# Keeping mixer tokens column by column of the grid, so that a neighbourhood attention reads 160 keys instead of 256

## The chip, the cores and the metric

The kernel runs on one core of one Trainium2 chip. The metric is the device time of one execution in microseconds (us). A time is the median of several runs; one further execution is taken by the hardware profiler, and what is read below of single instructions comes from that one.

## What is computed

Two layers of an encoder on 256 tokens of width 2048, all in 32-bit floats. Each layer has a mixing part with two attentions and a convolutional feed-forward part. Cut to what matters here:

```python
SEQ, GRID_W, NA_KH, NA_KW, WIN = 256, 64, 8, 16, 128     # 4 rows x 64 columns of tokens
h = rmsnorm(x, norm_mix[l]) * (1.0 + sc_a) + sh_a
qa, ka, va, qb, kb, vb, ga, gb = split_cols(h @ w_in[l])
ya = window_attention(qa, ka, va, sink_a[l]) @ w_proj_a[l]        # mixer A: |i - j| <= 128, with a sink
yb = neighbourhood_attention(qb, kb, vb, rel_bias_b[l]) @ w_proj_b[l]   # mixer B
merged = jax.nn.sigmoid(ga) * ya + jax.nn.sigmoid(gb) * yb
x = x + gt_a * (merged @ w_out[l])
# ... rmsnorm, w_up, depthwise conv over neighbouring tokens, silu gate, w_down
```

In mixer B (8 heads of 128) a query sees all 4 rows of the grid, and of the 64 columns a window of 16 that is moved inwards at the edges. A token's number is row * 64 + column. So in the usual order of tokens the keys that one query sees lie in four pieces, and every tile of 128 queries sees all 256 keys.

## The kernel before

**What streams.** Every weight matrix is cut into blocks of 128 x 128, and 16 blocks make a unit (1 MB, one DMA into a `raw` buffer). ScalarE (ACT) rounds each half unit to a high part (L326) and VectorE (DVE) subtracts it for the low part (L327); both land in an `hl` buffer. TensorE (PE) multiplies each block three times (high x high, high x low, low x high): `feature_block` (L343 to L345) with 256 tokens as moving columns, `tokens` (L406 to L408) with 512 output columns. Beside this stream the conditioning vectors are computed on DVE from `aw` tiles of 1 MB (L233). All DMAs of inputs are issued by one queue, SP, in program order: an issue that waits for a buffer holds back those behind it.

**The part around the change.** `normed` makes `h`, the normalised and modulated input, chunk by chunk (DVE L497, ACT L500, DVE L501), each chunk as high and low parts. From `h` come q, k, v of both mixers (`packs`) and the gates. A generator `attention` runs the 16 heads in steps between the matmuls of the stream; its pace is set by rates per unit. One head (`attend`) is: scores on PE into PSUM (L651); mask or bias added and the row's maximum taken on DVE (L654); exponential, sum and scaling on ACT (L662, L670); the probabilities turned so that keys lie on partitions; split into high and low parts (L418, L421); the sums of values on PE (L689); and the output split again (L691, L692). In layer 0 the scores are plain f32 matmuls and the turning is four PE transposes (L681) into PSUM. In layer 1 the scores are three split matmuls, and the turning is one DVE transpose of 32 x 32 blocks (L304), after which GpSimd (POOL) moves 16 blocks per head to their places (L298). For mixer B the tile `p` is first the bias, loaded by one DMA of 256 KB (L880), and then the probabilities. `merge` (L1011 to L1015) adds the gated outputs of both mixers and splits the sum; from there `w_out`, the residual and the feed-forward part follow. The pool `ev` has three buffers of the tag `z`, which `ht` in `normed` and `m` in `merge` use in turn.

**What sets the order.** The program is recorded in one go and a scheduler places the instructions of each engine by priorities and dependencies; each engine then runs its own in order. A few instructions are pinned in place (`keep_in_program_order`).

Of the kernel before, what the change touches and what calls it, by code (L numbers as in the profile page):

```python
# [9 lines left out]
F32 = mybir.dt.float32  # L10
F32R = mybir.dt.float32r
AF = mybir.ActivationFunctionType
# [3 lines left out]
P = 128  # L16
L = 2
D = 2048
S = 256
# [67 lines left out]

MOVED_QK = [(), (0,1,2,8)]
QK_STEPS = 3
MOVED = [(0,0), (8,8)]  # L90
STEPS = [1, 1]

ADA_ORDER = [[p * KC + k for k in range(KC) for p in ps] for ps in ((0, 1), (2,), (3, 4), (5,))]
# [48 lines left out]
def encoder(ctx: ExitStack, tc: tile.TileContext, a: dict, out: bass.AP):  # L142
# [43 lines left out]
    skip(96, const)  # L186
    skip(224)
    sp = pool("s", 1)

    def place(tag, n, dt, name):  # L190
        return sp.tile([P, n, S], dt, name=name, tag=tag)
# [110 lines left out]
    def turned_blocks(src, rows, n):  # L302
# [3 lines left out]
        dst = src.rearrange("p t (n k) -> p (t n k)", n=n).rearrange("p (n t k) -> p n t k", n=n, t=2)  # L306
        moved_blocks(dst, blocks)

    def unit_steps(l, u, by_halves=False):

        raw = rawp.tile([P, UB * P], F32, name=f"w{l}_{u}", tag="raw")
        if not by_halves:
            nc.sync.dma_start(raw[:], a["ws"][l, u])
        halves = []
        streamed = any(m == "w_in" and mo < GATE_A // P for m, _, mo in STREAMS[l][u * UB : (u + 1) * UB])
        at = OFF if streamed else 0
        for j in range(2):
            n = UB * P // 2  # L320
            hl = hlp.tile([P, 2 * n + ROW], F32R, name=f"hl{l}_{u}_{j}", tag="hl")
            hl = hl[:, at : at + 2 * n].rearrange("p (a n) -> p a n", a=2)
            r = raw[:, j * n : (j + 1) * n]
            if by_halves:
                nc.sync.dma_start(r, a["ws"][l, u][:, j * n : (j + 1) * n])
            nc.scalar.copy(hl[:, 0], r)  # L326
            nc.vector.tensor_tensor(out=hl[:, 1], in0=r, in1=hl[:, 0].bitcast(F32), op=ALU.subtract)  # L327
            halves.append(hl)
            if j == 0:
                yield halves  # L330
# [84 lines left out]
    def split(dst, src, scale=None, held=False):  # L415
# [9 lines left out]
            out=dst[:, 1], in0=src, scalar=scale, in1=dst[:, 0].bitcast(F32), op0=ALU.mult, op1=ALU.subtract  # L425
        )

    def half_tanh(dst, src, **kw):

        nc.scalar.activation(out=dst, in_=src, func=AF.Tanh, scale=0.5, **kw)  # L430
# [60 lines left out]
    def normed(l, w, h, rbs):  # L491

        mod, amod = mods[l], amods[l]
        for kc in range(KC):
            t = ev.tile([P, S], F32, name="ht", tag="z")
            sh = mod[:, 3 * w * KC + kc : 3 * w * KC + kc + 1]
            nc.vector.scalar_tensor_tensor(  # L497
                out=t[:], in0=x[:, kc], scalar=amod[:, w, kc : kc + 1], in1=rbs[:], op0=ALU.mult, op1=ALU.mult
            )
# [145 lines left out]

    def attend(q, k, v, p, mask, scale, sink, o, rows=None):

        sc = ax.tile([P, 2, S], F32, name="sc", tag="ax")
        for t in range(2):
            for i, j in by(q):  # L650
                nc.tensor.matmul(sc[:, t], q[i][:, t * P : (t + 1) * P], k[j], start=i + j == 0, stop=(i, j) == by(q)[-1])  # L651
        m = sm.tile([P, 2], F32, name="m", tag="m")
        for t in range(2):
            nc.vector.tensor_tensor_reduce(  # L654
                out=p[:, t], in0=sc[:, t], in1=mask[:, t], scale=scale, scalar=-3.0e38 if sink is None else sink,
                op0=ALU.add, op1=ALU.max, accum_out=m[:, t : t + 1],
            )
        nm = sm.tile([P, 2], F32, name="nm", tag="nm")
        nc.vector.tensor_scalar(out=nm[:], in0=m[:], scalar1=-1.0, scalar2=None, op0=ALU.mult)
        den = sm.tile([P, 2], F32, name="den", tag="den")  # L660
        for t in range(2):
            nc.scalar.activation(out=p[:, t], in_=p[:, t], func=AF.Exp, bias=nm[:, t : t + 1], accum_out=den[:, t : t + 1])  # L662
        if sink is not None:
            es = sm.tile([P, 2], F32, name="es", tag="es")
            nc.scalar.activation(out=es[:], in_=nm[:], func=AF.Exp, bias=sink)
            nc.vector.tensor_tensor(out=den[:], in0=den[:], in1=es[:], op=ALU.add)
        ri = sm.tile([P, 2], F32, name="ri", tag="ri")
        nc.vector.reciprocal(out=ri[:], in_=den[:])
        for t in range(2):
            nc.scalar.activation(out=p[:, t], in_=p[:, t], func=AF.Copy, scale=ri[:, t : t + 1])  # L670
        yield
        if rows is not None:
            turned_blocks(p[:], rows(), 2)
            for _ in range(STEPS[sink is None]):
# [8 lines left out]
        split(pT, tp[:], held=rows is not None)  # L683
        v = v()
        yield
        po = ax.tile([P, 512], F32, name="po", tag="ax")
        for i, j in by(v):
            for b in range(2):
                nc.tensor.matmul(po[:, :S], v[i][:, b], pT[:, j, b], start=i + j + b == 0, stop=i + b == 2)  # L689
# [96 lines left out]
    def small(l):  # L786

        if l == 0:
            tables.extend((load(a["maskA"], [P, 2, S], "maskA"), load(a["cs"], [P, 2, 2, HALF], "cs")))
        cs = tables[1]  # L790
        gains = load(a["gains"][l], [P, 4], f"gains{l}", lay, tag="gains", bufs=1)
        rg = load(a["rg"][l], [P, 2, ROT], f"rg{l}", lay, tag="rg", bufs=1)
        sink = load(a["sink"][l], [P, HA], f"sink{l}", lay, tag="sink", bufs=1)
        cw = load(a["cw"][l], [P, 2 * FC, 4], f"cw{l}", lay, tag="cw", bufs=1)
        nc.vector.tensor_scalar(out=gains[:, 2:3], in0=gains[:, 2:3], scalar1=SCALE, scalar2=None, op0=ALU.mult)
        rots = []
        for w in range(2):
            rot = lay.tile([P, 4, 2, HALF], F32, name=f"rot{l}_{w}", tag=f"rot{w}", bufs=1)
            for i, (f, g) in enumerate(((0, 0), (1, 1), (0, 1), (1, 0))):
                nc.vector.tensor_tensor(  # L800
                    out=rot[:, i], in0=cs[:, f],
                    in1=rg[:, w, g * HALF : (g + 1) * HALF].unsqueeze(1).broadcast_to([P, 2, HALF]), op=ALU.mult,
                )
            rots.append(rot)

        return gains, sink, cw, rots

    for l in range(L):
# [17 lines left out]
        if l:  # L826


            def bare_gate(mo):
                def evac(ps):  # L830
                    z, sh = bare.level(ps, 0.5)
                    half_tanh(ya[:, mo], z[:], bias=sh[:, :1])
# [17 lines left out]
        def head_a(i):  # L850
# [21 lines left out]
            yield from attend(  # L872
                q, k, v, p, tables[0], SCALE, sink[:, i : i + 1], lambda: oA[i], rows if i < MOVED[l][0] else None
            )

        def head_b(hb):
            b, i = packs[1 + hb // 4], hb % 4
            v = b[:, 4:8].rearrange("p (t a) s -> p t (a s)", t=2)
            p = at.tile([P, 2, S], F32, name="p", tag="p")
            nc.sync.dma_start(p[:], a["bias"][l, hb])  # L880
            q = in_halves(b[:, 8 + i], f"qB{l}_{hb}", "qh", l in SCORES_3)
            k = in_halves(b[:, i], f"kB{l}_{hb}", "kh", l in SCORES_3)
            yield
            yield from attend(
                q, k, lambda: in_halves(v[:, :, i * HEAD : (i + 1) * HEAD], f"vB{l}_{hb}", "vh", True), p, p, 1.0, None,
                lambda: oB_of(hb), (lambda: b[:, i : 9 + i : 8]) if hb < MOVED[l][1] else None,
            )

        def oB_of(hb):
# [119 lines left out]
        for mo in range(KC):  # L1009

            def merge(ps):  # L1011
                z = ev.tile([P, S], F32, name="m", tag="z")
                gated(z[:], gb[mo], ps)
                nc.vector.tensor_tensor(out=z[:], in0=z[:], in1=ya[:, mo], op=ALU.add)
                split(merged[mo], z[:], 0.5)  # L1015

            st.features(oB, [merge])

# [185 lines left out]
```

## Time and profile before

| | |
|---|---|
| time, median of 3 runs | 2653.98 us (2653.2 to 2656.04) |
| profiled execution, its own time | 2661.45 us |
| its span, first to last instruction | 2659.6 us |
| TensorE clock granted | 1.000 of full speed |
| busy: PE, DVE, ACT, POOL | 99%, 80%, 53%, 9% of the span |
| DMA | 700.42 MB, 70.8% of 16 engines' time for the SP queue |

The profiled execution is 7.5 us above the median of the plain runs, and 1.85 us of its time lie outside the span. A row of a group gives line, engine, operation, tiles and shapes, count, then busy time in us, mean ns of one, and the idle time just before with its cause. In the timeline a row gives start, duration, engine and line; where several instructions were merged, the count stands at the end. The duration of one matmul is longer than the distance to the next, since matmuls overlap: their price is the distance of starts. The profile records each plain f32 matmul as two (32 rows for the 16 f32 score matmuls of the 8 B heads in layer 0).

### The profile page before, as it was taken

Reading aid. Unit: us, or ns where it says so; the run is one execution under the profiler, and the core shown is the slowest. Engines: PE = TensorE matmul, PEld = TensorE weight load, DVE = VectorE, ACT = ScalarE, POOL = GpSimd, SP = SyncE. Lnnn points to the kernel's source line nnn. Section 1 sums busy time; section 2 is a strip of 40 time slices with the busy share of each in tenths; the row PEclk is TensorE's granted clock in tenths of the full one; section 3 lists DMA queues with packets and bytes.
Section 4 is the critical chain, followed back from the end, with each engine's and each line's share of the span. In section 5 each row is a group of like instructions: output and inputs, shape, how many; then the busy total and the mean of one; then the engine's idle time right before and its main releaser. Section 6 shows DMA issues by size and latency. Waiting matters only on the chain.

```text
span 2659.6 us, 51014 instructions
## 1 busy us (share of the span) xinstructions
PE 2643.3 (99%) x21164; PEld 2557.9 (96%) x21164; DVE 2121.0 (80%) x2979; ACT 1408.9 (53%) x2280; POOL 228.2 (9%) x345
## 2 busy tenths in 40 slices
PE   9999999999999999999999999999999999999999
PEld 7888899999999999999998889999999999999999
DVE  8898998997987888788886778868888866655664
ACT  5445865456643555355554666654565445544553
POOL 0001100000000000000002558520000000000000
PEclk9999999999999999999999999999999999999999
DMA  9987779885777777877766666666747765555554
GB/s 371 349 329 292 267 294 356 316 339 184 295 272 289 284 287 285 306 296 285 283 221 253 249 234 232 253 258 257 283 178 287 297 252 191 192 196 194 196 191 143
DMA packets 102042, 700.42 MB, mean 263 GB/s; under 512 B 12721, under 2 KB 15025, under 8 KB 17969
## 3 DMA queue, kind: packets, MB, share of 16 engines
q1 hardware_dynamic: 101810, 697.17, 70.8%
q8 instruction: 165, 2.70, 0.4%
q14 instruction: 67, 0.55, 0.1%
HBM read 695.03 MB, written 2.10 MB: 262 GB/s over the span
## 4 chain that ended last, share of the span: by engine, by line
PE 86%; DMA 5%; DVE 5%; issue 2%; ACT 1%; POOL 0%; SPq 0%; DVEq 0%; ACTq 0%
PE ps L343 24%; PE ps L345 24%; PE ps L344 24%; DMA aw<-in_aw 4%; PE ps_t L408 4%; PE ps_t L407 4%; PE ps_t L406 4%; DVE hl L327 2%; DVE aw L233 1%; PE sc L651 1%; ACT hl L326 1%; PE po L689 1%; DMA w<-in_ws 1%; DVE u L1049 0%; POOL qrs L472 0%
## 5 line engine op out<-in xcount | busy, mean ns | idle before, releaser
L327 DVE TENSOR_TENSOR hl<-w,hl 128x1024 fp32r<-128x1024 f32 x928 | 1129.8, 1224 | 298.0 <-ACT hl L326 294.7
L326 ACT CAST hl<-w 128x1024 fp32r<-128x1024 f32 x928 | 969.8, 1049 | 719.7 <-PE ps L345 501.4
L343 PE MATMUL ps<-h,hl 128*128 128x256 f32 x3328 | 922.4, 277 | 1.3 <-DVE ya L970 0.6
L344 PE MATMUL ps<-h,hl 128*128 128x256 f32 x3328 | 919.6, 276 | 0.0
L345 PE MATMUL ps<-h,hl 128*128 128x256 f32 x3328 | 919.6, 277 | 0.0
L343 PEld LDWEIGHTS ps<-h,hl 128*128 128x128 f32 x3328 | 624.7, 188 | 2.4 <-DVE ya L970 0.8
L344 PEld LDWEIGHTS ps<-h,hl 128*128 128x128 f32 x3328 | 625.3, 188 | 0.4 <-DVE h L501 0.2
L345 PEld LDWEIGHTS ps<-h,hl 128*128 128x128 f32 x3328 | 624.4, 188 | 0.0
L233 DVE CUSTOM_DVE_ANT_0 aw<-aw,cact,ab 128x2048 f32<-128x2048 f32 x189 | 443.8, 2349 | 92.5 <-DMA aw<-in_aw 91.7
L406 PE MATMUL ps_t<-hl,h 128*128 128x512 f32 x576 | 223.0, 392 | 2.7 <-ACT h L500 2.0
L407 PE MATMUL ps_t<-hl,h 128*128 128x512 f32 x576 | 225.0, 391 | 0.3
L408 PE MATMUL ps_t<-hl,h 128*128 128x512 f32 x576 | 224.3, 390 | 0.0
L1049 DVE SCALAR_TENSOR_TENSOR u<-ps,cw,u 128x255 f32<-128x255 f32 x304 | 146.0, 480 | 62.0 <-ACT u L1047 58.1
L1047 ACT ACTIVATE u<-ps,cw 128x256 f32<-128x256 f32 x152 | 85.7, 564 | 155.4 <-PE ps L345 155.2
L343 PE MATMUL ps<-act_o,hl 128*128 128x256 f32 x512 | 142.0, 278 | 2.7 <-DVE u L1049 2.6
L345 PE MATMUL ps<-act_o,hl 128*128 128x256 f32 x512 | 142.1, 278 | 1.3 <-DVE hl L327 1.3
L344 PE MATMUL ps<-act_o,hl 128*128 128x256 f32 x512 | 142.0, 277 | 0.0
L345 PE MATMUL ps<-merged,hl 128*128 128x256 f32 x512 | 141.5, 277 | 0.0
L344 PE MATMUL ps<-merged,hl 128*128 128x256 f32 x512 | 141.5, 276 | 0.0
L343 PE MATMUL ps<-merged,hl 128*128 128x256 f32 x512 | 141.5, 277 | 0.0
L406 PEld LDWEIGHTS ps_t<-hl,h 128*128 128x128 f32 x576 | 107.9, 188 | 26.1 <-ACT h L500 3.0
L407 PEld LDWEIGHTS ps_t<-hl,h 128*128 128x128 f32 x576 | 108.1, 188 | 23.9 <-DVE hl L327 1.9
(244 smaller groups left out, 4800.3 us busy)
## 6 DMA issues: line engine op xcount, KB each, us to landing
w<-in_ws SPq DMA_DIRECT2D x463, 1024.0 KB, 4.9
aw<-in_aw SPq DMA_DIRECT2D x189, 1024.0 KB, 6.3
p<-in_bias SPq DMA_DIRECT2D x16, 256.0 KB, 4.5
x<-in_xT SPq DMA_DIRECT2D x4, 512.0 KB, 5.5
aw_o<-in_aw SPq DMA_DIRECT2D x2, 1024.0 KB, 12.4
out<-x SPq DMA_DIRECT2D x16, 128.0 KB, 3.2
w<-in_ws SPq DMA_DIRECT2D x2, 512.0 KB, 11.8
aw_b<-in_aw SPq DMA_DIRECT2D x1, 1024.0 KB, 18.1
```

The costliest lines, as they stand in the source:

```text
L233: nc.vector.tensor_tensor_reduce(out=raw[:], in0=raw[:], in1=cact[:], scale=1.0, scalar=ab[:, i : i + 1], op0=ALU.mult, op1=ALU.add, accum ...
L326: nc.scalar.copy(hl[:, 0], r)
L327: nc.vector.tensor_tensor(out=hl[:, 1], in0=r, in1=hl[:, 0].bitcast(F32), op=ALU.subtract)
L343: nc.tensor.matmul(out, hi, act[0], start=first, stop=False)
L344: nc.tensor.matmul(ps[:, :S], hi, act[1], start=False, stop=False)
L345: nc.tensor.matmul(out, lo, act[0], start=False, stop=last)
L406: nc.tensor.matmul(ps[:], xh, hi, start=kc == kcs[0], stop=False)
L407: nc.tensor.matmul(ps[:], xh, lo, start=False, stop=False)
L408: nc.tensor.matmul(ps[:], xl, hi, start=False, stop=kc == kcs[-1])
L651: nc.tensor.matmul(sc[:, t], q[i][:, t * P : (t + 1) * P], k[j], start=i + j == 0, stop=(i, j) == by(q)[-1])
L1047: nc.scalar.activation(out=u, in_=ps, func=AF.Identity, scale=w[:, 1:2], bias=w[:, 3:4])
L1049: nc.vector.scalar_tensor_tensor(out=u[:, to], in0=ps[:, of], scalar=w[:, j : j + 1], in1=u[:, to], op0=ALU.mult, op1=ALU.add)
```

## The change

From `normed` to `merge` the tokens stand column by column: a token's number there is column * 4 + row. `normed` for the mixing part writes its first product in that order (reading `x` row by row, writing with a step of four elements), so that q, k, v, gates and both attentions follow. `merge` writes its sum back in row order, with a step of 64 elements, and into a second `z` tile instead of in place. The eight gates of layer 1 that are made ahead of `h` are written in column order by the ACT instruction that makes them. Tables indexed by token (the mask of mixer A, the rotary table, the bias of mixer B) are loaded by `load_tokens` in four DMAs each (the rotary table in two times four), which place the query tokens; the keys in mixer A's mask are turned once by two POOL copies, and the bias of B is read with a step by L654's successor.

In this order the first 128 queries see only keys 0 to 159 and the last 128 only keys 96 to 255 (NEAR = 160). Mixer B's scores, maximum, exponential, scaling, turning and split take 160 keys per tile. The sums of values accumulate in one PSUM tile of 256 columns: the first matmul of the first 128 keys writes columns 0 to 159, the first of the last 128 keys is cut in two (columns 96 to 159 are added, 160 to 255 are fresh), and the others have 160 columns: seven matmuls per head instead of six. The probabilities no longer overwrite the bias but the head's own k and q in `packs`; in layer 0 POOL sets the 96 unseen columns of each tile to zero before the PE transposes, in layer 1 POOL moves 12 smaller pieces per head instead of 16.

```diff
+GRID_H = S // GRID_W
+NEAR = P + BLOCK
...
+    def load_tokens(dst, src):
+        rows = src.rearrange("(q w c) h f -> w q c h f", q=GRID_H // 2, w=2)
+        for w in range(2):
+            for q in range(GRID_H // 2):
+                nc.sync.dma_start(dst[q::2, w], rows[w, q])
...
+    def turned_near(p, turned):
+        nc.vector.transpose(out=near(turned), in_=near(p))
+        for a in range(P // BLOCK):
+            for d in (-1, 0, 1):
+                ...
+                nc.gpsimd.tensor_copy(out=to, in_=of)
...
+            to, of, roots = (t[:], x[:, kc], rbs[:]) if w else (columns_by_row(t[:]), by_rows(x[:, kc]), by_rows(rbs[:]))
             nc.vector.scalar_tensor_tensor(
-                out=t[:], in0=x[:, kc], scalar=amod[:, w, kc : kc + 1], in1=rbs[:], op0=ALU.mult, op1=ALU.mult
+                out=to, in0=of, scalar=amod[:, w, kc : kc + 1], in1=roots, op0=ALU.mult, op1=ALU.mult
             )
...
-                nc.tensor.matmul(sc[:, t], q[i][:, t * P : (t + 1) * P], k[j], start=i + j == 0, stop=(i, j) == by(q)[-1])
+                nc.tensor.matmul(
+                    sc[:, t, :n], q[i][:, t * P : (t + 1) * P], k[j][:, part(t)], start=i + j == 0, stop=(i, j) == by(q)[-1]
+                )
...
+        if window and rows is None:
+            nc.gpsimd.memset(sheared(p, NEAR, -NEAR, S - NEAR), 0.0)
...
-                nc.tensor.matmul(po[:, :S], v[i][:, b], pT[:, j, b], start=i + j + b == 0, stop=i + b == 2)
+                fresh = window and b == 1 and i + j == 0
+                for c in (slice(S - n, n), slice(n, S)) if fresh else (part(b),):
+                    nc.tensor.matmul(po[:, c], v[i][:, b], pT[:, j, b, c], start=i + j + b == 0, stop=i + b == 2)
...
-            nc.sync.dma_start(p[:], a["bias"][l, hb])
+            load_tokens(p[:], a["bias"][l, hb])
...
-                nc.vector.tensor_tensor(out=z[:], in0=z[:], in1=ya[:, mo], op=ALU.add)
-                split(merged[mo], z[:], 0.5)
+                both = ev.tile([P, S], F32, name="m2", tag="z")
+                nc.vector.tensor_tensor(
+                    out=rows_by_column(both[:]), in0=by_columns(z[:]), in1=by_columns(ya[:, mo]), op=ALU.add
+                )
+                split(merged[mo], both[:], 0.5)
```

On PE, where the stream passes from `w_proj_a` to the second gate in layer 0, stood before the value sums of B's head 3 (`vB_3`), the transposes of head 4's probabilities (`tp`) and the scores of head 5 (`sc`):

```order
L344 MATMUL ps_60_8_0_3900<-oA_7_2940,hl_59_1_3872 128x256
L345 MATMUL ps_60_8_0_3900<-oA_7_2940,hl_59_1_3872 128x256
L689 MATMUL po<-pT,vB_3_3716 128x256 x6
L681 MATMUL tp<-ident,p 128x128 x4
L651 MATMUL sc<-packB_1_225 128x256 x2
L343 MATMUL ps_60_16_0_3972<-h_0_171,hl_60_0_3975 128x256
```

and stands now:

```order
L394 MATMUL ps_60_8_0_3939<-oA_7_2953,hl_59_1_3911 128x256
L772 MATMUL po<-pT,vB_3_3751 128x160
L772 MATMUL po<-pT,vB_3_3751 128x64
L772 MATMUL po<-pT,vB_3_3751 128x96
L772 MATMUL po<-pT,vB_3_3751 128x160 x4
L759 MATMUL tp<-ident,packB_1_225 128x128 x4
L715 MATMUL sc<-packB_1_225 128x160 x2
L392 MATMUL ps_60_16_0_4016<-h_0_171,hl_60_0_4019 128x256
```

The place in the stream is the same; the value sums are seven pieces instead of six, and the transposes keep their size.

On DVE, in the first merges of layer 0 (`m` and `merged`, between the low parts `hl` of units 77 to 79 and one conditioning tile `aw_67`), stood before:

```order
L434 SCALAR_TENSOR_TENSOR m<-gb_y_3967,ps_77_8_0_5097 128x256
L1014 TENSOR_TENSOR m<-m,ya_222 128x256
L327 TENSOR_TENSOR hl_78_1_5204<-w_78_5199,hl_78_1_5204 128x1024
L424 SCALAR_TENSOR_TENSOR merged_5058<-m,merged_5058 128x256
L434 SCALAR_TENSOR_TENSOR m<-gb_y_3967,ps_77_16_0_5127 128x256
L1014 TENSOR_TENSOR m<-m,ya_222 128x256
L233 ISA aw_67_5329,mod_172<-aw_67_5329,cact,ab_173 128x2048
```

and stands now:

```order
L491 SCALAR_TENSOR_TENSOR m<-gb_y_4011,ps_77_8_0_5151 128x256
L376 TENSOR_TENSOR hl_78_1_5261<-w_78_5256,hl_78_1_5261 128x1024
L1106 TENSOR_TENSOR m_5178<-m,ya_222 128x64x4
L491 SCALAR_TENSOR_TENSOR m<-gb_y_4011,ps_77_16_0_5182 128x256
L473 SCALAR_TENSOR_TENSOR merged_5111<-m_5178,merged_5111 128x256
L1106 TENSOR_TENSOR m_5217<-m,ya_222 128x64x4
L376 TENSOR_TENSOR hl_79_0_5328<-w_79_5326,hl_79_0_5328 128x1024
L473 SCALAR_TENSOR_TENSOR merged_5111<-m_5217,merged_5111 128x256
L268 ISA aw_67_5389,mod_172<-aw_67_5389,cact,ab_173 128x2048
```

The number of instructions per merge is the same; the sum now goes to a tile of its own with a step, and a low part of the weights has moved by a place.

On the SP queue, at the tables of layer 0, behind unit 15 of the weights, stood before:

```order
L315 DMA w_15_974<-in_ws 128x2048
L178 DMA maskA<-in_maskA 128x512
L178 DMA cs<-in_cs 128x64
L178 DMA gains_992<-in_gains 128x4
L178 DMA rg_994<-in_rg 128x64
L178 DMA sink_996<-in_sink 128x8
L178 DMA cw_998<-in_cw 128x352
L232 DMA aw_17_1033<-in_aw 128x2048
L315 DMA w_16_1037<-in_ws 128x2048
```

and stands now:

```order
L364 DMA w_15_974<-in_ws 128x2048
L223 DMA seen<-in_maskA 64x256 x4
L223 DMA cs<-in_cs 64x1x16 x8
L181 DMA gains_1005<-in_gains 128x4
L181 DMA rg_1007<-in_rg 128x64
L181 DMA sink_1009<-in_sink 128x8
L181 DMA cw_1011<-in_cw 128x352
L267 DMA aw_17_1046<-in_aw 128x2048
L364 DMA w_16_1050<-in_ws 128x2048
```

Twelve issues stand where two stood, ahead of the next conditioning tile and the next unit of weights.

More of the change, by code (lines that the diff above doesn't have):

```diff
@@ L89 @@
 QK_STEPS = 3
-MOVED = [(0,0), (8,8)]
+MOVED = [0, 8]
+WINDOWS_FROM = [8, 0]
 STEPS = [1, 1]
@@ L426, in split, with split_near @@
         )
+    def split_near(dst, src, held):
+        high, low = near(dst[:, 0]), near(dst[:, 1])
+        copied = nc.scalar.copy(high, near(src))
+        if held:
+            tc.keep_in_program_order(copied)
+        nc.vector.tensor_tensor(out=low, in0=near(src), in1=high.bitcast(F32), op=ALU.subtract)
     def half_tanh(dst, src, **kw):
@@ L646, in attend, with part @@
     def attend(q, k, v, p, mask, scale, sink, o, rows=None):
+        window = sink is None
+        n = NEAR if window else S
+        def part(t):
+            return slice(t * (S - n), t * (S - n) + n)
         sc = ax.tile([P, 2, S], F32, name="sc", tag="ax")
@@ L661, in attend @@
         for t in range(2):
-            nc.scalar.activation(out=p[:, t], in_=p[:, t], func=AF.Exp, bias=nm[:, t : t + 1], accum_out=den[:, t : t + 1])
+            e = p[:, t, part(t)]
+            nc.scalar.activation(out=e, in_=e, func=AF.Exp, bias=nm[:, t : t + 1], accum_out=den[:, t : t + 1])
         if sink is not None:
@@ L669, in attend @@
         for t in range(2):
-            nc.scalar.activation(out=p[:, t], in_=p[:, t], func=AF.Copy, scale=ri[:, t : t + 1])
+            e = p[:, t, part(t)]
+            nc.scalar.activation(out=e, in_=e, func=AF.Copy, scale=ri[:, t : t + 1])
+        if window and rows is None:
+            nc.gpsimd.memset(sheared(p, NEAR, -NEAR, S - NEAR), 0.0)
         yield
         if rows is not None:
-            turned_blocks(p[:], rows(), 2)
-            for _ in range(STEPS[sink is None]):
+            if window:
+                turned_near(p, mask)
+            else:
+                turned_blocks(p, rows(), 2)
+            for _ in range(STEPS[window]):
                 yield
@@ L682, in attend @@
         pT = at.tile([P, 2, 2, S], F32R, name="pT", tag="pT", bufs=1)
-        split(pT, tp[:], held=rows is not None)
+        if window:
+            split_near(pT, tp, rows is not None)
+        else:
+            split(pT, tp[:], held=rows is not None)
         v = v()
@@ L788, in small @@
         if l == 0:
-            tables.extend((load(a["maskA"], [P, 2, S], "maskA"), load(a["cs"], [P, 2, 2, HALF], "cs")))
+            seen = at.tile([P, 2, S], F32, name="seen", tag="p")
+            load_tokens(seen[:], a["maskA"])
+            mask = const.tile([P, 2, S], F32, name="maskA")
+            for t in range(2):
+                nc.gpsimd.tensor_copy(out=by_columns(mask[:, t]), in_=rows_by_column(seen[:, t]))
+            cs = const.tile([P, 2, 2, HALF], F32, name="cs")
+            for f in range(2):
+                load_tokens(cs[:, f], a["cs"][:, f])
+            tables.extend((mask, cs))
         cs = tables[1]
@@ L831, in evac @@
                     z, sh = bare.level(ps, 0.5)
-                    half_tanh(ya[:, mo], z[:], bias=sh[:, :1])
+                    half_tanh(columns_by_row(ya[:, mo]), by_rows(z[:]), bias=sh[:, :1])
                 return evac
```

33 lines of the change are left out of this document (29 added, 4 removed).

## The prediction

> **What bounds the kernel now.** I read the page first, then PE's share of windows, then single stretches of the timeline. From the page, the busy times and the chain that ended last:
>
> ```profile
> PE 2643.3 (99%) x21164; PEld 2557.9 (96%) x21164; DVE 2121.0 (80%) x2979; ACT 1408.9 (53%) x2280; POOL 228.2 (9%) x345
> PE 86%; DMA 5%; DVE 5%; issue 2%; ACT 1%; POOL 0%; SPq 0%; DVEq 0%; ACTq 0%
> ```
>
> PE is the bound nearly everywhere. So an edit pays or costs in two ways only: PE's own rate, or a place where PE comes to wait. Windows tell how near DVE, the next engine, is to that (window, length, then busy time of PE, PEld, DVE, ACT, POOL):
>
> ```profile
> 340.00:390.00 50.00, 50.00 (x406) 48.27 (x405) 47.88 (x91) 31.18 (x62) 0.00 (x0) 1.00 0.83 306
> 390.00:450.00 60.00, 60.00 (x519) 59.69 (x518) 54.47 (x80) 31.83 (x57) 0.00 (x0) 1.00 0.96 360
> 491.00:512.00 21.00, 21.00 (x186) 21.00 (x185) 20.49 (x33) 10.65 (x16) 0.00 (x0) 1.00 0.83 304
> 512.00:534.00 22.00, 22.00 (x194) 22.00 (x193) 22.00 (x40) 11.87 (x21) 0.00 (x0) 1.00 0.72 271
> 534.00:560.00 26.00, 26.00 (x231) 26.00 (x230) 25.05 (x45) 13.67 (x25) 0.00 (x0) 1.00 0.83 317
> 560.00:620.00 60.00, 60.00 (x528) 60.00 (x527) 52.57 (x73) 31.53 (x46) 0.00 (x0) 1.00 0.83 314
> 1800.00:1822.00 22.00, 22.00 (x195) 22.00 (x194) 20.02 (x34) 11.44 (x17) 0.00 (x0) 1.00 0.65 247
> 1822.00:1846.00 24.00, 24.00 (x212) 24.00 (x211) 23.71 (x44) 13.45 (x27) 0.00 (x0) 1.00 0.72 269
> ```
>
> The first two hold B's heads of layer 0, the third and fourth the merges of layer 0, the last two those of layer 1. In all of them PE is busy throughout: nothing is to be won there by making DVE or ACT faster. In the merges of layer 0 DVE is full (22.00 of 22): there more DVE work can make PE wait.
>
> **Term 1: scores in layer 0.** On PE's timeline stand four records of plain f32 scores (one head), six value sums and six split scores, one-column matmuls, and 128-column f32 ones:
>
> ```profile
> 376.06 1.03 PE L651 MATMUL sc<-packB 128*128 128x256 f32 x4
> 376.74 0.47 PE L343 MATMUL ps<-oA,hl 128*128 128x256 f32 x1
> 377.05 0.28 PE L344 MATMUL ps<-oA,hl 128*128 128x256 f32 x1
> ```
> ```profile
> 1622.12 0.84 PE L689 MATMUL po<-pT,vA 128*128 128x256 f32 x6
> 1622.80 0.84 PE L651 MATMUL sc<-kB,qB 128*128 128x256 f32 x6
> 1623.48 0.28 PE L343 MATMUL ps<-h,hl 128*128 128x256 f32 x1
> ```
> ```profile
> 1934.65 0.50 PE L461 MATMUL ssm<-mean,sq 128*128 128x1 f32 x4
> 1935.01 0.36 PE L343 MATMUL ps<-bare_a,hl 128*128 128x258 f32 x1
> ```
> ```profile
> 13.68 2.92 PE L441 MATMUL warm<-ident 128*128 128x128 f32 x24
> 16.44 0.38 PE L479 MATMUL rb<-ident,nrs 128*128 128x128 f32 x2
> ```
>
> A split matmul of 256 columns takes (1623.48 - 1622.80) / 6 = 0.113 us. Between 376.06 and 377.05 lie the four f32 scores and one such matmul, so a score record takes (0.99 - 0.113) / 4 = 0.22. At 128 columns f32 takes (16.44 - 13.68) / 24 = 0.115, so at 160, a quarter of the way, 0.14. There are 8 heads x 4 = 32 records: 32 x 0.08 = **-2.5 us**; at 0.115 it would be -3.4, and with the price in proportion to columns (0.1375) -2.6.
>
> **Term 2: value sums, and split scores in layer 1.** One column costs (1935.01 - 1934.65) / 4 = 0.09 and 128 cost 0.115: with weights of 128 x 128 to load each time, a matmul has a floor near 0.1 that columns don't lower. So I take 0.113 for 160, 96 and 64 columns alike. The 48 split scores of layer 1 then gain nothing, and one value sum more per head costs 16 x 0.113 = **+1.8 us** (1.4 at the lowest row, 0.09). The trace has no split matmul of fewer than 256 columns; both ends are rivals below.
>
> **Term 3: less work for DVE, ACT and POOL in B's heads.** Of the groups (busy us and mean ns at the end):
>
> ```profile
> L327 DVE TENSOR_TENSOR hl<-w,hl 128x1024 fp32r<-128x1024 f32 x928 | 1129.8, 1224 | 298.0 <-ACT hl L326 294.7
> L298 POOL COPY p<-packB 32x128 f32<-32x128 f32 x128 | 77.8, 608 | 35.5 <-DVE packB L304 17.7 <-issue 11.4 <-POOL p L298 1.3
> L497 DVE SCALAR_TENSOR_TENSOR ht<-x,amod,rbs 128x256 f32<-128x256 f32 x64 | 28.8, 477 | 0.5
> L1014 DVE TENSOR_TENSOR m<-m,ya 128x256 f32<-128x256 f32 x32 | 13.5, 421 | 0.3
> L654 DVE CUSTOM_DVE_ANT_0 p<-sc,p 128x256 f32<-128x256 f32 x32 | 12.3, 418 | 2.9 <-DMA p<-in_bias 2.7 <-PE sc L651 0.2
> L418 ACT CAST pT<-p 128x512 fp32r<-128x512 f32 x16 | 10.0, 626 | 0.0
> ```
>
> An element costs DVE (1224 - 421) / 768 = 1.05 ns, so 96 fewer in each of two reductions and 192 fewer in the split save 0.4 us per head, 0.6 in layer 1 with the transpose: 8 us in all. POOL moves 96 smaller pieces instead of 128 of 608 ns. All of it is worth **0**, since PE does not wait in these windows, and ACT's pinned split (last row, idle 0.0) does not wait for POOL. By the same cover the new waits are free: in layer 0 the first reduction overwrites k and must wait for the whole head's scores, with low parts (L327) queued behind it, some 0.3 us; POOL's zeroing ends before the two ACT passes that also precede the transposes; and on SP the bias loads of later heads, freed earlier, now stand ahead of a weight unit and wait for a reduction. Without that cover, 0.3 us x 8 = 2.4.
>
> **Term 4: steps in memory.** `normed` writes every fourth element (32 instructions of L497's form), `merge` every 64th (32 of L1014's). No row shows such an access, so the bounds are the price unchanged and each element twice: + 256 x 1.05 = 0.27 us an instruction. I take the middle, 0.13, as no row is nearer to either. For the start, the chain of waits:
>
> ```profile
> 33.98 0.50 DVE ht L497
> 45.38 0.49 DVE ht L497
> 56.79 0.49 DVE ht L497
> 68.78 0.50 DVE ht L497
> ```
>
> Four stand on the chain: 4 x 0.13 = **+0.5 us** (0 to 1.1; 16 x 0.27 = 4.3 were all 16 of layer 0 on it). Merges, layer 0: 16 x 0.13 = 2.1 us against DVE's idle 0.51 + 0 + 0.95 = 1.46 up to 560: **+0.7** (0 to 4.3 - 1.5 = 2.8). Layer 1: 2.1 against 1.98 + 0.29 = 2.27: **0** (0 to 2.0). What is left drains behind, where DVE has 7.4 us idle (560 to 620). The step in the bias (a reduction of 160 elements, at worst 168 ns longer than now planned) lies under term 3's cover, and so do the eight gates of layer 1 that ACT writes with a step and POOL's two copies of mixer A's mask, made long before A's first head.
>
> The merge also adds a wait. With two of the three `z` tiles per merge, the gating product of the next merge but one needs a tile that the low part of this merge still reads, and that low part waits for ACT, where it stands behind casts of weights. What queues behind it on DVE are the next low parts `hl`, and PE waits for those. I take 0, because DVE runs its queue in order and the low part stands ahead of that product anyway; if ACT is late by one cast (about 1 us), it costs at most that once per layer, 2 us, since the casts run ahead of PE.
>
> The Trainium skill (Advanced Engine Details and Errata, Memory Cachelines) says that an access which meets a different 16-byte line for each element pays a penalty. Both steps are of that kind, so by it the upper ends would hold; no run here shows it yet.
>
> **Term 5: twelve issues on SP instead of two.** SP's timeline, and the next weights' arrival:
>
> ```profile
> 96.52 0.43 SPq L178 DMA_DIRECT2D maskA<-in_maskA  x1
> 99.08 0.45 SPq L178 DMA_DIRECT2D cw<-in_cw  x1
> 100.74 0.33 SPq L232 DMA_DIRECT2D aw<-in_aw  x1
> 103.04 0.33 SPq L315 DMA_DIRECT2D w<-in_ws  x1
> 105.31 0.33 SPq L232 DMA_DIRECT2D aw<-in_aw  x1
> ```
> ```profile
> 110.54 1.05 ACT L326 CAST hl<-w 128x1024 fp32r<-128x1024 f32 x1 [3.60 <-DMA w<-in_ws]
> 115.06 1.22 DVE L327 TENSOR_TENSOR hl<-w,hl 128x1024 fp32r<-128x1024 f32 x1
> ```
>
> Ten more at 0.45 are 4.5 us, of which 100.74 - 99.53 = 1.2 was waiting: the tile `aw` goes out 3.3 us later, the unit of weights 1.5, the `aw` behind it on time. ACT's first cast of that unit waited for the DMA until 110.54, but its low part came only at 115.06 by DVE's queue: 115.06 - 111.59 = 3.5 us of cover. **+0.3 us** as an estimate (0 to 3.3, if the cover is gone).
>
> **Sum.** -2.5 + 1.8 + 0.5 + 0.7 + 0.3 = +0.8 us on the profiled execution's 2661.45, which is 2662.3. That execution lies 7.5 above the median of plain runs; the same change on 2653.98 gives **2654.8 us**. A measurement of this kernel tells about 0.2% (5.3 us) from no change.
>
> **Rivals.**
> *Steps cost double, and DVE holds PE up.* It decides from the point where an add in layer 0's merges is 1.46 / 16 = 0.09 us longer. Price: start 1.1 to 4.3, merges 2.8 + 2.0; with the other terms (-2.5 + 1.8 + 0.3) +5.5 to +8.7, 2659.5 to 2662.7, say 2661: slower. For: DVE at 22.00 of 22. Against: idle just before and behind.
>
> *Split matmuls under 256 columns run at f32's rate.* Two records of 0.14 = 0.28 instead of 0.113 for 48 + 80 matmuls of 160 columns, +21.7; 32 short ones at 0.23, +3.7: 2680. For: none so short has been seen. Against: 256 and 258 columns show no edge.
>
> *Columns alone set the price.* 0.113 x 160/256 = 0.071: 48 x 0.042 = 2.0 saved in the scores; value sums of 960 instead of 1536 columns, 0.42 a head instead of 0.79, 5.9 saved: +0.8 - 7.9 = -7.1, 2646.9. For: in f32, 256 columns cost 0.22 and 128 cost 0.115. Against: 0.09 for one column, which leaves the weights' load as the floor.
> The Trainium skill (TensorE: Matmul & The Clock Gate, Back-to-back issue gap) gives a lone matmul N / 2.4 + 2.5 ns, 69 ns for 160 columns, an estimate that would bring 2646.7; the one-column row, far above that formula, speaks against it.
>
> **Chances.** Forecast 0.56 (0.48 within 0.2%, 0.04 each side for a reordered stall), double steps 0.22 (0.18 slower, 0.04 same), f32 rate 0.10, columns alone 0.12. Faster 0.16, same 0.52, slower 0.32. Range 2646 to 2663: forecast, double steps and columns alone, 0.9 less their outer parts; the f32 rate is left out.
>
> **What would show it.** Right: scores `sc` in layer 0 near 0.14 apart; seven value sums in 0.79 us; `m` and `ht` near 550 and 610 ns; PE without waits between 491 and 560. Wrong: split matmuls of 160 columns at 0.07 or above 0.2 us, `m` at 690 ns with PE waiting for `hl`, or PE idle near 116 for the late unit.

## The result, and the profile after

The changed kernel takes 2693.64 us (median of four runs, 2689.06 to 2695.59) against 2654.82 for the kernel before: ratio 1.0145, interval 1.0129 to 1.0161. It is 1.45% slower, well outside the forecast range of 2646 to 2663. Of the profiled executions, the one before took 2661.45 us (7 above its median) and the one after 2689.06 (5 below), so the traces show 27.6 of the 38.8 us between the medians.

The page of the kernel after, busy times and chain:

```profile
PE 2651.6 (99%) x21180; PEld 2564.5 (95%) x21180; DVE 2123.4 (79%) x2979; ACT 1402.1 (52%) x2280; POOL 202.2 (8%) x323
PE 84%; DVE 7%; issue 3%; ACT 2%; POOL 2%; DMA 2%; SPq 0%; POOLq 0%; DVEq 0%; ACTq 0%
```

DVE, ACT and POOL have hardly more to do than before, and still PE's share of the chain fell from 86% to 84% and DVE's rose from 5% to 7%: somebody waits. The window that holds layer 1's B heads shows where; first before, then after (window, length, busy time of PE, PEld, DVE, ACT, POOL, then granted clock, DMA share, GB/s):

```profile
1640.00:1800.00 160.00, 160.00 (x1405) 160.00 (x1404) 122.11 (x184) 90.12 (x160) 79.14 (x132) 1.00 0.68 253
```
```profile
1640.00:1800.00 160.00, 144.03 (x1188) 143.00 (x1187) 101.39 (x171) 74.04 (x144) 48.51 (x101) 0.95 0.55 205
```

PE stood still for 16 us there, its clock was lower, every other engine did less too, and the DMAs moved less. That is what a queue that holds everybody back would look like. Who waits on SP in that window, in the kernel before:

```profile
SPq L880 <- DVE pT L421: 5.1, 7, 1.2
```

and after (L223 issues the bias, L267 `aw`, L364 the weights; total us, times, longest):

```profile
SPq L223 <- POOL packB L356: 41.4, 6, 10.0
...
SPq L223 <- DVE p L346: 8.7, 2, 4.4
```

The bias load of a later head now waits for POOL's piece copies, because the change uses the bias tile as scratch for the 32 x 32 transposes (`turned_near(p, mask)`, where `mask` is the bias tile): the tile is free only after POOL's last piece. In the kernel before it was free even later, for there POOL's pieces land in it and the split (L421) reads them; but the load stood further back. Seven of the eight bias loads of layer 1 now have 1 to 6 units of weights fewer ahead of them on SP. So it is the earlier place and the wait for POOL together that hold SP; the runs below take the wait away, and none moves the load back. One turn of the loop, from the timelines of POOL, SP, DVE and PE of the kernel after:

```profile
1659.67 6.67 POOL L356 COPY packB<-p 32x32 f32<-32x32 f32 x12 [12.40 <-DVE amod L275]
...
1666.38 2.39 SPq L223 DMA_DIRECT2D p<-in_bias  x4
1668.87 1.05 SPq L364 DMA_DIRECT2D w<-in_ws  x1
1670.01 0.38 SPq L267 DMA_DIRECT2D aw<-in_aw  x1
...
1676.89 2.35 DVE L268 CUSTOM_DVE_ANT_0 aw<-aw,cact,ab 128x2048 f32<-128x2048 f32 x1 [7.35 <-DMA aw<-in_aw]
1679.17 1.22 DVE L376 TENSOR_TENSOR hl<-w,hl 128x1024 fp32r<-128x1024 f32 x1
...
1680.45 0.58 PE L394 MATMUL ps<-oA,hl 128*128 128x256 f32 x1 [5.57 <-DVE hl L376]
```

POOL ends at 1666.34; at once SP issues the bias, then the weights and `aw` that stood behind it. DVE stands 7.35 us at `aw`, the low part `hl` stands behind that, and PE waits 5.57 us for it. A late DVE makes the next transpose late, and so the next pieces on POOL, and so the next bias load: POOL sat idle 67.2 us here waiting for that transpose.

PE pays for each such stop twice. Windows of the same trace behind that wait:

```profile
1680.40:1684.00 3.60, 3.55 (x16) 3.56 (x17) 3.60 (x6) 0.00 (x0) 0.00 (x0) 0.50 0.82 328
1684.00:1688.00 4.00, 4.00 (x29) 4.00 (x27) 2.59 (x4) 2.37 (x6) 0.00 (x0) 0.73 0.96 336
1688.00:1692.00 4.00, 4.00 (x37) 4.00 (x36) 2.87 (x12) 2.00 (x9) 0.00 (x0) 1.00 1.00 397
```

The granted clock is 0.50 when PE starts again: 16 matmuls in 3.6 us instead of 32. The three long stops (3.8, 5.7 and 6.2 us) were followed by 3.0, 4.9 and 5.9 us at 0.213 us per matmul instead of 0.113. The Trainium skill (TensorE: Matmul & The Clock Gate, What you observe and What's actually happening) states that an idle window of about 3.4 us halves PE's clock until it has been busy for about as long. The halving agrees with these rows; two of the three recoveries are longer than that, and in e3_bias_one_load (below) a stop of 2.5 us was enough for 5.9 us at half the clock. Counted by the start of each n-th matmul on streamed weights, PE fell 26 us behind the kernel before between 1650 and 1800.

The second loss is at the start. SP's timeline, then PE's:

```profile
97.53 2.46 SPq L223 DMA_DIRECT2D seen<-in_maskA  x4
100.04 5.66 SPq L223 DMA_DIRECT2D cs<-in_cs  x8
...
108.17 0.36 SPq L267 DMA_DIRECT2D aw<-in_aw  x1
108.64 1.27 SPq L364 DMA_DIRECT2D w<-in_ws  x1
...
121.19 0.73 PE L455 MATMUL ps_t<-hl,h 128*128 128x512 f32 x2 [3.44 <-ACT hl L375]
122.45 0.50 PE L456 MATMUL ps_t<-hl,h 128*128 128x512 f32 x1 [0.53 <-DVE hl L376]
```

The twelve issues take 8.2 us, `aw` goes out at 108.17 instead of 100.74, and PE stands still for 3.4 us from 117.7 on, then runs at half the clock from 123 to 126: 6.1 us lost between 100 and 150, where the kernel before lost nothing.

The sizes that the prediction asked for, from the groups (busy us, mean ns) and from PE's timeline in layer 0:

```profile
L555 DVE SCALAR_TENSOR_TENSOR ht<-x,amod,rbs 128x256 f32<-128x256 f32 x64 | 34.5, 579 | 0.5
L1106 DVE TENSOR_TENSOR m<-m,ya 128x256 f32<-128x256 f32 x32 | 20.2, 631 | 0.3
L725 DVE CUSTOM_DVE_ANT_1 packB<-sc,p 128x160 f32<-128x160 f32 x32 | 13.0, 437 | 7.3 <-DMA p<-in_bias 6.8 <-PE sc L715 0.5
```
```profile
361.26 0.44 PE L715 MATMUL sc<-packB 128*128 128x160 f32 x2
361.54 0.49 PE L759 MATMUL tp<-ident,packB 128*128 128x128 f32 x3
...
363.95 0.99 PE L772 MATMUL po<-pT,vB 128*128 128x160 f32 x7
364.78 0.32 PE L392 MATMUL ps<-oA,hl 128*128 128x256 f32 x1
```

`m` rose from 421 to 631 ns. Half of the `ht` instructions write with a step, so the mean of 579 against 477 is +0.20 us for each of those. A reduction of 160 elements takes 437 ns where 256 took 418. The read of the bias is the only access in it with a step, so probably that read eats what the shorter row saves; no run here takes it out. An f32 score record is 0.14 from the next, seven value sums take 0.83 us.

### The profile page after: what moved, and what is told of

It is laid out like the page before. It is cut to its first block, busy times and chain, and to the rows that moved or that the text cites. A ratio compares the mean times of both kernels' runs of the same rounds, so it can differ in the third digit from the quotient of the medians.

```text
span 2687.2 us, 51133 instructions
## 1 busy us (share of the span) xinstructions
PE 2651.6 (99%) x21180; PEld 2564.5 (95%) x21180; DVE 2123.4 (79%) x2979; ACT 1402.1 (52%) x2280; POOL 202.2 (8%) x323
## 4 chain that ended last, share of the span: by engine, by line
PE 84%; DVE 7%; issue 3%; ACT 2%; POOL 2%; DMA 2%; SPq 0%; POOLq 0%; DVEq 0%; ACTq 0%
PE ps L392 24%; PE ps L394 24%; PE ps L393 24%; PE ps_t L456 4%; PE ps_t L457 4%; PE ps_t L455 4%; DVE hl L376 2%; DVE aw L268 2%; DMA aw<-in_aw 1%; ACT hl L375 1%; POOL packB L356 1%; PE sc L715 1%; PE po L772 0%; POOL packB L333 0%; POOL p L333 0%
## 6 DMA issues: line engine op xcount, KB each, us to landing
aw_o<-in_aw SPq DMA_DIRECT2D x2, 1024.0 KB, 12.5
```

## Experiments

Theory A: on SP, loads that PE needs stand behind something that SP waits for or has to issue; in layer 1 the bias load that waits for POOL, at the start ten more issues. Theory B: it is the number of issues everywhere, the four per bias too. Theory C: ACT's pinned split of the probabilities waits for POOL's pieces, and the casts of weights behind it are late.

### Four single edits

**Own scratch.** The transpose writes to slots of the previous head:

```diff
-                turned_near(p, mask)
+                turned_near(p, rows())        # packs, slots of head hb - 1; for hb = 0 two slots of qTa
```

> Only layer 1's B heads change: the 32 x 32 transposes on DVE write to two slots of the previous head that are free by then, no longer over the bias tile, so a later bias load waits for this head's reductions on DVE and not for its 12 piece copies on POOL. The result is the same. Theory A (on SP the bias load stands waiting for POOL, 41.4 us in six waits, with `aw` and `w` loads behind it; DVE then stands at `aw`, the low parts behind it, PE at those): the 26 us of PE between 1650 and 1800 come back, 2693.6 - 26 = about 2668, and SP's waits for POOL are gone. Theory B (four issues per bias keep SP for 2.4 us each, and that alone makes the weights late): 2692 to 2695. Theory C (ACT's pinned split, which waits for POOL's pieces, holds up the casts behind it): 2692 to 2695.

2664.56 us (2664.18 to 2670.36), ratio to before 1.0045 (1.0028 to 1.0062): 29 us come back, where A said 26, and neither B nor C allows it. The order on SP is the same but for one unit of weights that goes out some places later; what changed is whom SP waits for, in the same window as above:

```profile
SPq L223 <- DVE nm L730: 10.0, 4, 2.6
SPq L223 <- DVE m L725: 0.9, 1, 0.9
```

These are the reductions that the prediction had thought the load waits for. PE is busy for 159.98 of the 160 us.

**Tables in one load each,** in the new order already in memory:

```diff
-            load_tokens(seen[:], a["maskA"])
-            ... two POOL copies, and for the rotary table two times load_tokens
+            tables.extend((load(a["maskA"], [P, 2, S], "maskA"), load(a["cs"], [P, 2, 2, HALF], "cs")))
```

> Mixer A's mask and the rotary table come from memory already in the new token order, with one load each, so the ten extra issues near 97 to 106 us and POOL's two copies of the mask are gone; all else is the kernel after. Theory A (the issues hold SP until 106, `aw` and `w` go out 7 us later than before, ACT waits 4.5 us for `w`, PE 3.6 + 0.7, and PE's clock drops to 0.97 in that window): 2693.6 - 6 = about 2687.5, and no gap of PE near 117. Rival (the gap comes from DVE's stepped writes of h, which hold up the chain there): 2692 to 2694, with the gap still there.

2683.06 us (2682.4 to 2687.66), ratio 1.0112 (1.0097 to 1.0127): 10.6 less, more than the 6 expected. The gap near 117 is gone and PE loses nothing between 100 and 150, which is 6.1; the other 4.5 have no place in the two traces and lie within the spread of the kernel after, whose runs reach from 2689 to 2696.

**The bias in one load:**

```diff
-            load_tokens(p[:], a["bias"][l, hb])
+            nc.sync.dma_start(p[:], a["bias"][l, hb])
```

> The bias comes from memory with its queries already in the new order, one load of 256 KB per head instead of four of 64 KB, in both layers; POOL's pieces, the scratch and all else as in the kernel after. Theory A (the load waits for POOL, however many issues it has): the waits of SP for POOL stay and only 1.8 us of issuing per head go, 2685 to 2691. Theory B (the issues alone): 16 x 1.8 = 29 us less of SP's time, layer 1's loss gone, about 2668. Theory C: 2692 to 2695.

2690.07 us (2688.29 to 2695.41), ratio 1.0138 (1.0123 to 1.0153): B's 2668 is far off. One issue waits as long as four:

```profile
SPq L971 <- POOL packB L356: 43.4, 6, 11.4
```

The nearly equal times hide two moves that cancel by luck. Between 1650 and 1800 PE lost 18 us here instead of 26, so three issues less per bias are worth up to 8 us as long as the load stands behind POOL; with the own scratch they are worth 0.4 at most (1.6 us lost there in e5_three_undone below, 2.0 in e1_own_scratch). And in the merges of layer 0 (490 to 557) PE lost 6.1 us instead of 1.6, where this edit had moved `aw` to other places on SP.

**PE turns in layer 1** as it does in layer 0:

```diff
-WINDOWS_FROM = [8, 0]
+WINDOWS_FROM = [8, 8]
```

> Layer 1's B heads are turned as layer 0's are: POOL zeroes the corner and PE does four transposes of 128 columns per head; no DVE transposes, no POOL pieces, no scratch. Bias loads stay four issues each. PE pays 8 x 4 x 0.115 = +3.7 us. Theory A: the 26 us come back, 2693.6 - 26 + 3.7 = about 2671. Theory B: 2693.6 + 3.7 = 2697. Theory C: the split no longer waits for POOL, so about 2671 as well; against e1_own_scratch it tells A from C.

2670.19 us (2669.79 to 2672.54), ratio 1.0061 (1.0046 to 1.0076). As A and C said; 5.6 above the own scratch, of which 2.9 are PE's 32 transposes. The rest is not explained by the edit: its profiled execution lost 3.9 us more than that of e1_own_scratch in the merges of layer 0, which the edit does not touch.

### POOL's time: none, once, twice

The order on SP is the same in all three; only the number of copies per piece differs.

```diff
-                nc.gpsimd.tensor_copy(out=to, in_=of)
+                for _ in range(2):                                # e6; e12: no copy
+                    nc.gpsimd.tensor_copy(out=to, in_=of)
```

> The kernel after, with each of POOL's 96 piece copies in layer 1's B heads made twice (the second writes the same values), some 6 us more per head. Theory A (SP stands until POOL's last piece, loads behind it): each of the six waits grows by 4 to 6 us and PE pays for it, 2693.6 + 25 to 36 = 2719 to 2730. Rival (the loss has to do with where the loads stand on SP, not with how long POOL takes): 2692 to 2698.

> The kernel after without POOL's 96 piece copies in layer 1's B heads: the transposed blocks stay in the bias tile and the 32 x 32 blocks of p are not exchanged, so mixer B of layer 1 is left incomplete. The order on SP is that of the kernel after and of e6_pieces_twice: 0, 1 and 2 copies per piece. Theory A: with no copy the bias load waits for a DVE transpose only, the 26 us of layer 1 come back, 2663 to 2670, against 2693.6 with one copy and 2706.3 with two. Rival (it is the tile's sharing with the transpose on DVE, not POOL's time, that counts): 2680 or more.

> e1_own_scratch with each piece copied twice. Theory A (without the shared tile POOL is off the path, ACT's pinned split has cover): 2664.6 to 2668. Theory C (the pinned split waits for POOL and holds up the casts behind it): 8 heads x about 6 us, 2690 or more.

None: 2667.72 us (2666.3 to 2669.8), ratio 1.005 (1.0036 to 1.0064). Twice: 2706.32 (2703.29 to 2707.33), ratio 1.0194 (1.0179 to 1.021). Twice with the own scratch: 2666.13 (2665.14 to 2666.37), ratio 1.0041 (1.0027 to 1.0055). SP's waits for the bias tile, with no copy, with two (its window reaches to 1830), and what waits for POOL with two copies and the own scratch:

```profile
SPq L223 <- DVE p L346: 18.3, 4, 5.4
```
```profile
SPq L223 <- POOL packB L357: 55.6, 6, 13.4
```
```profile
ACT pT L481 <- POOL packB L357: 13.6, 6, 3.3
```

SP's wait for POOL of 0, 41.4 and 55.6 us goes with 2667.7, 2693.6 and 2706.3 us: 0.6 to 0.9 us for each of its us. Theory A holds, though twice the copies cost 13 us and not the 25 to 36 expected: SP's wait grew by 14.2 us only. Part of the longer copying fell into time in which POOL had stood waiting for the late DVE (67.2 us with one copy, 55.8 with two, between 1640 and 1800). Theory C falls: with the own scratch, ACT's pinned split did wait 13.6 us for POOL, and the whole cost was 1.6 us over e1_own_scratch; between 1650 and 1800 PE lost 2.1 us, against 2.0 there. It also rules out that POOL's work as such slows PE or DVE down: POOL copies twice as much there.

### Undone together

> The edits of e1_own_scratch, e2_tables_one_load and e3_bias_one_load together; the rest of the change (160 keys, new token order, stepped writes, seven value sums) stays. Theory A (three separate losses on SP's queue): 2664.6 - 10.6 = 2654.0, and up to 3.6 less for the bias issues: 2650 to 2654, no measurable difference from the kernel before. What is then left of the change is its own sum: -2.5 + 1.8 for PE's columns, about +2.5 for the stepped writes. Rival (the rest of the change costs by itself, each edit only uncovered another wait): above 2660.

2667.98 us (2663.31 to 2669.27), ratio 1.0044 (1.0032 to 1.0057): 14 above what A said. PE wins 5.2 us at the start over e1_own_scratch and loses 6 between 412 and 557. In layer 0, between 400 and 560, DVE waits for `aw`:

```profile
DVE aw L268 <- DMA aw<-in_aw: 19.2, 13, 3.5
```

In e2_tables_one_load the same wait is 1.9 us there. With one load for the bias the scheduler had put `aw` and the tables of layer 1 in other places on SP and DVE. So that edit was left out:

> The edits of e1_own_scratch and e2_tables_one_load, the bias in four loads as in the kernel after, so that layer 0's queues keep the order they have in e2_tables_one_load (in e5_three_undone the one-load bias had moved `aw` on SP and DVE in layer 0, and 6.3 us were lost between 412 and 557). Theory A (two separate losses that add): 2664.6 - 10.6 = 2654.0, within 0.2% of the kernel before. Rival (startup and layer 0 are coupled: what is won at 117 is lost again in the gates and merges of layer 0, whatever the bias does): 2660 or more.

2659.63 us (2658.45 to 2662.81), ratio 1.0019 (1.001 to 1.0028): just below the rival's 2660, and 5.6 above A's sum. Own scratch and tables win 34 of the 39 us. The rival's reason is not what the traces show: what is won at the start is kept, for PE is 5.9 us ahead of e1_own_scratch at 134 and still 5.5 at 620. A's sum was wrong in its second term: it took the whole 10.6 for the tables, of which the traces had shown 6.1. With 6.1 it gives 2658.5, 1.1 below the measured time, so the two edits add.

One run more told the issues from POOL's copies of the mask:

> e1_own_scratch, with mixer A's mask and the rotary table in one load each (their rows come in the new token order), and POOL's two copies that turn the mask's columns kept: against e9_two_undone it has only those copies more, against e1_own_scratch only the ten issues less. Theory A (the issues on SP make the weights late near 117): no gap of PE near 117, the time of e9_two_undone, 2658 to 2661. Rival (POOL's two copies of 2.1 us, at 103 to 107, slow DVE's low parts or hold back the rotary tables): the gap stays, 2664 to 2665.

2660.92 us (2658.43 to 2666.6), ratio 1.0022 (1.0012 to 1.0032). Window 100 to 150 of e1_own_scratch, then of this kernel:

```profile
100.00:150.00 50.00, 46.04 (x201) 37.52 (x200) 43.58 (x57) 19.36 (x23) 3.94 (x2) 0.97 0.80 304
```
```profile
100.00:150.00 50.00, 50.00 (x231) 41.77 (x231) 47.90 (x62) 22.08 (x26) 3.94 (x2) 1.00 0.94 347
```

POOL's copies are there in both (3.94 us), the gap only with the issues. So it was the issues.

### The stepped add

```diff
-                both = ev.tile([P, S], F32, name="m2", tag="z")
-                nc.vector.tensor_tensor(
-                    out=rows_by_column(both[:]), in0=by_columns(z[:]), in1=by_columns(ya[:, mo]), op=ALU.add
-                )
+                nc.vector.tensor_tensor(out=z[:], in0=z[:], in1=ya[:, mo], op=ALU.add)
...
+            to, of = (by_rows(x[:, mo]), columns_by_row(ps)) if part == 2 else (x[:, mo], ps)
```

> e5_three_undone, and the return to row order is taken out of the merge (its add is again in place, 256 neighbouring elements) and put into the residual add behind w_out, which reads its PSUM bank with a step of 4 elements and writes x in order. Theory A (the stepped add of +0.21 us, sixteen times in layer 0 where DVE has no idle time, costs PE 1.6 to 6 us): m back at 421 ns, no gap of PE near 540, 2 to 6 us under e5_three_undone, 2646 to 2651. If a stepped read of PSUM costs the same +0.21, it falls where DVE has idle time and costs nothing more. Rival (the stage near 540 waits for something else): the same time as e5_three_undone.

> e9_two_undone with the return to row order moved from the merge's add to the residual add behind w_out, as in e8_step_in_residual. If the stepped add (+0.21 us, sixteen times) is what makes PE wait near 540, that gap of 1.4 us goes and the runs that lose 5 us more there go with it: 1.5 to 5 us under e9_two_undone, 2649 to 2653. Rival (something else sets that stage, as e8_step_in_residual hinted, where 4.2 us were lost between 490 and 557 with m at 421 ns): no difference, 2653 to 2655.

On e5_three_undone: 2663.09 us (2661.83 to 2668.93), ratio 1.0034 (1.0023 to 1.0046), 4.9 less; as many as A said, but not where A said: between 490 and 557 PE stands still for 4.2 us in both traces. Of the 6.0 us between the two traces, 0.7 lie at the start, 2.1 from 412 to 490, where there is no merge, and 3.4 between 750 and 900, where the matmuls of e5_three_undone stood further apart (last section). On e9_two_undone: 2659.14 (2657.59 to 2661.76), ratio 1.0019 (1.001 to 1.0028), no difference; both expected times were too low, since they were reckoned from A's 2654. Two groups of the latter:

```profile
L1102 DVE TENSOR_TENSOR m<-m,ya 128x256 f32<-128x256 f32 x32 | 13.5, 421 | 0.3
L1111 DVE SCALAR_TENSOR_TENSOR x<-ps,mod,x 128x256 f32<-128x256 f32 x128 | 60.1, 480 | 26.7 <-PE ps L394 26.2
```

The add is back at 421 ns, and the residual adds take 480 against 479 before; the 32 of them that now read PSUM with a step take 480 by themselves, so that step costs nothing. The gap of 1.4 us at 535 went, and PE stopped 0.8 us at 559 and 1.1 at 592 instead, for low parts. DVE stood waiting ahead of both, between 545 and 600:

```profile
DVE aw L268 <- DMA aw<-in_aw: 6.9, 3, 2.9
```

In e9_two_undone that wait is 4.6 us (500 to 600), in the kernel before 1.5 (535 to 600). The rival won: the step itself is not what decides here, and late `aw` tiles again stand ahead of the low parts that PE waits for. Why they are late here, no run settles.

## Why the prediction was wrong

**The step that failed is in term 3: "By the same cover the new waits are free".** The prediction saw that the bias loads of later heads now stand further forward on SP (it said ahead of "a weight unit"; it is up to six), but had them "wait for a reduction". The wait it read was right for own scratch (10.9 us on SP in e1_own_scratch, which PE hardly feels) and wrong for the change: the bias tile is also the target of the transpose, so the load waits for POOL's last piece, 41.4 us in six waits, and PE pays 26 to 29 us. The tile's last reader was in the code of the change, in one argument (`turned_near(p, mask)`); the description of the change leaves this use of the bias tile out. The price without cover, 0.3 us x 8 = 2.4, was that of low parts behind a reduction on DVE; nothing priced SP's queue. The other half of the sentence, that ACT's pinned split does not wait for POOL, held in effect: even a wait of 13.6 us cost 1.6 at most.

**Term 5** had the right place (PE idle near 116 was its sign of being wrong) and was too small: 0.45 us an issue where the twelve took 8.2 / 12 = 0.68, so that `aw` was 7.4 us late and not 3.3 (1.0 of it because the whole start was later), and the cover of 3.5 us was gone. +0.3 became 3.6 to 4.9 us by the medians (e13_copies_kept and e9_two_undone against e1_own_scratch), 6.1 in the traces.

**Terms 1 and 2** were right in kind and size. A last score record stands only 0.03 us ahead of the matmul behind it, which then takes longer, so that matmul is counted with each group here, less its usual 0.113. The 32 score records of layer 0 then take 4.4 us in e9_two_undone instead of 6.9 (-2.5, as forecast), the 112 value sums 12.5 instead of 11.3 for 96 (+1.1, forecast +1.8), the 48 split scores of layer 1 5.6 instead of 5.5. The sum is -1.3 against -0.7. The rivals "f32's rate" and "columns alone" fell with it: a split matmul of 160 columns stands 0.109 us from the next on average, not 0.28 or 0.071. (In the first of these rivals 128 x 0.167 is 21.4, not 21.7; its 2680 stands.)

**Term 4** took half of a doubling; the steps cost +0.20 and +0.21, nearer to the upper end (0.27). The start became about 1.0 us later (forecast 0.5), and layer 0's merges 1.6 (forecast 0.7); but e10_two_undone_step_in_residual, without the step there, loses 2.5 just behind, so the 1.6 are not shown to be the step's. The Trainium skill (Advanced Engine Details and Errata, Memory Cachelines) states a penalty for such accesses, without a size, and these rows agree for writes to SBUF at a step of 16 and of 256 bytes.

What is left with both queue losses undone, 2659.6, lies near where the rival of the double steps stood (2661), but taking the step out of the merges won nothing. By the start of each n-th matmul on streamed weights, e9_two_undone falls behind the trace of before by 1.0 us until 134, 0.3 until 446, 1.7 until 551, 0.6 until 620 and 1.7 in layer 1's heads and behind them: 5.3 together, against 5.2 between the medians (7.7 us that the trace of before alone lost between 750 and 1350 are left out). In layer 0's heads PE's own gain of about 2 was thus given back. Small waits that the kernel before does not have make up 1.2 of it: transposes for ACT's scaling of the probabilities (0.8), one other transpose for a reduction (0.2) and a value sum for a low part on DVE (0.2). The prediction had put the waits in these heads at nothing. What holds up ACT and DVE there, and where the rest went, no run here settles. No version beat the kernel before.

## What to carry to other kernels

When a tile gets a second use, list its last reader on every engine, and look at where its next load stands and at what stands behind it: on a queue that runs in order, that load's wait is everybody's wait. A new DMA issue has two prices, its own time on the queue and the lateness of all behind it, to be set against the cover that the next consumer has. And a stop of PE can cost more than its own length: here, when the clock was halved behind it, half of the recovery time came on top.

## What the hardware showed that was not expected

- After stops of 3.8 to 6.2 us PE ran at half its clock for 3.0 to 5.9 us; after stops of up to 2.0 us its rate did not change. In between the length alone does not decide: one stop of 2.5 us (e3_bias_one_load, 1665) was followed by 5.9 us at half the clock, one of 2.8 us (the kernel before, 782) by none.
- SP's issues are not of one price: 0.33 us for a load of weights, of `aw` or of a whole bias, 0.43 to 0.57 for the small tables of the kernel before that go out one behind the other, about 0.6 for each piece of a bias (2.39 to 2.40 for most of the fours), of the mask and of the rotary table (whose 5.66 us hold a pause of 0.7).
- A read of PSUM by DVE with a step of 16 bytes was free (480 ns against 479), a write of 256 elements to SBUF with a step of 16 or 256 bytes cost 0.20 to 0.21 us.
- The floor under short matmuls is not a fixed distance. Of a head's value sums in e1_own_scratch, the matmul of 64 columns started 0.072 us after one of 160, that of 96 columns 0.067 after it, and the next 0.129 later: together 0.09 each, while 160 columns in a row stood 0.112 apart.
- In the profiled execution of before, and in that of e5_three_undone, matmuls stood 0.118 us apart instead of 0.113 from about 800 to 870 (in the first of them from 782 on, right behind a stop of 2.8 us), at a granted clock of 1.00 and with no wait of PE to explain it; the profiled executions of the other kernels do not show it there. Its cause is open.
